# One-core diffusion backbone: attention threaded piece by piece through its projections, a third output unit ahead, idle products removed

## The chip, the cores and the metric

The program runs on one core of a Trainium2 chip. The metric is the time of one execution on the device in microseconds (us), median of several runs. TensorE multiplies matrices, VectorE and ScalarE do elementwise work, GpSimd is almost unused, and SyncE issues the loads. The profile calls them PE (with PEld for its weight loads), DVE, ACT, POOL and SP.

## The reference, cut to what matters

The model has two layers over 256 latent tokens and 256 context tokens of width 1024. Layer 0 is: half FFN, differential attention, half FFN; layer 1 has a Hyena convolution in the middle. Everything is float32. The change is inside the attention of layer 0:

```python
def attend(q, k, v):
    s = jnp.einsum('bqhmd,bkhmd->bhmqk', q, k).astype(jnp.float32)
    p = jax.nn.softmax(s, axis=-1)
    a = (p[:, :, 0] - lam_full * p[:, :, 1]).astype(v.dtype)
    return jnp.einsum('bhqk,bkhe->bqhe', a, v)
...
of = of * lax.rsqrt(jnp.mean(of * of, -1, keepdims=True) + LN_EPS)
of = of * subln_g.astype(jnp.float32) * (1.0 - lam_init)
return of.astype(o.dtype).reshape(b, n, DA_HEADS * DA_V_DIM) @ w_o
```

There are 8 heads, each with two softmaxes over 512 keys; queries and latent keys are rotated (rope). Only the 256 latent tokens have queries. After `w_o` comes a gated residual and a layer norm, then the next half FFN.

## The kernel before, in words

A float32 product is made of three TensorE products of rounded parts: each operand is split into a high part (ScalarE cast, `wH`, `qh`, `aH`) and a remainder (VectorE subtraction, `wL`, `ql`, `aL`), and high x high, high x low and low x high are summed in a PSUM bank. Weights come in units of 1 MB: two landing buffers (`raw`), three split units (`wH`/`wL`). `Stream` splits the next unit as soon as one is given back with `st.done`.

The attention works on two heads at a time, t = 0 to 3. For each t there are three projections, each with a weight unit of its own: queries (`pq`, 48 products of 256 columns), keys (`pka`, `pkb`, 48 products of 512 columns) and values (`pv`, 96 products of 256 columns). From them come, for each of two heads (hd) and two blocks of 128 queries (qt), a score block `sc`: two PSUM banks, one for each softmax, six products that use half of the array's rows each, so that two can run side by side. VectorE takes the row maximum (`mx`, L1035), ScalarE the exponential and its sum (`prob`, L1037), VectorE combines the two softmaxes (L1040 to L1044). The result is transposed on TensorE (`at`, L1062), split (`aH`, `aL`), multiplied with the values (`po`), squared and summed (`oss`), normed (`oe`, `odg`, and the product `orb` that spreads the factor over partitions), and split again (`oh`): two of the eight inputs of the output projection. That projection (`Project`, `py`) has four weight units of two output tiles each. Each tile is added to the residual `zl` (L1182), and `Norm` sums up the layer norm's statistics (`lnpm`, `lnd`, `lnq`, `lndl`, `lnst`, `lnrb`) tile by tile; `Norm.pilot` subtracts a first mean from all eight tiles as soon as the first tile is done.

The order inside a stage is not written out: the program is written in one order, and a list scheduler places each instruction by priority and by its own estimate of when operands are ready. On the chip each engine then runs its list strictly in that order. There are 7 PSUM banks for all of this and one more for `adaps` and `fill`. In the order of writing, all four score blocks of a t come as one call (`scores`), `values(t - 1)` takes parts of a projection between its steps (`part`, `V_BOUNDS`), and two units of the output projection are opened ahead.

`fill(n)` (L493) adds n products of a matrix of ones with itself, into a bank that nobody reads. It is called five times with n = 20: after each layer norm but the last. Being of low priority and waiting for nothing, all 100 were placed by the scheduler wherever it estimated TensorE to be free. Each is a float32 product that runs in two passes, so the trace has 200 records.

Of the kernel before, what the change touches and what calls it, by code (L numbers as in the profile page):

```python
# [33 lines left out]
ADA_LATER = 75  # L34
FILL = 20
# [15 lines left out]
V_BOUNDS = (0, 3, 5, 8)  # L51
# [253 lines left out]
def backbone(ctx, tc, A, out):  # L305
# [596 lines left out]
    fill(FILL)  # L902


    def attention(X, rope):
# [73 lines left out]
        def proj_qk(t, between=None):  # L979
            qi, pq, qo = q_outs()  # L980
            gemm(qo, XL, KT)
            st.done(qi)
            q_end(t, pq)
            if between:
                between()
            ki, pk, ko = k_outs()
            gemm(ko, X, KT)
            st.done(ki)
            k_end(t, pk)

        def proj_v(t):
            vi = st.get("w")
            pv = [bank("pv"), bank("pv")]
            v_mm(vi, pv, 0, KT)
            st.done(vi)
            v_end(t, pv)

        def first():
            qi, pq, qo = q_outs()
            ki, pk, ko = k_outs()  # L1000
            vi = st.get("w")
            pv = [bank("pv"), bank("pv")]
            ks = 5
            for k in range(ks):
                gemm(qo, XL, KT, k, k + 1)
                gemm(ko, X, KT, k, k + 1)
                v_mm(vi, pv, k, k + 1)
            gemm(qo, XL, KT, ks)
# [5 lines left out]
            v_mm(vi, pv, ks, KT)  # L1014
            st.done(vi)
            v_end(0, pv)

        def scores(t):
            qh, ql = Q.pop(t)
            kk = K.pop(t)  # L1020
            rec = sm(4, "rec")
            AA[t] = ([], rec)
            for hd in range(2):
                kh, kl = kk[hd]
                for qt in range(2):
                    ps = [bank("sc"), bank("sc")]
                    c = slice(T * hd + P * qt, T * hd + P * qt + P)
                    for n, (q2, k2) in enumerate(((qh, kh), (qh, kl), (ql, kh))):
                        for m in range(2):
                            r = slice(64 * m, 64 * m + 64)  # L1030
                            nc.tensor.matmul(ps[m], q2[r, c], k2[r, :], start=n == 0, stop=n == 2,  # L1031
                                             skip_group_check=True, tile_position=(64 * m, 0))
                    mx, sums, pr = sm(2, "mx"), sm(2, "sums"), []
                    for m in range(2):
                        V.tensor_reduce(mx[:, m:m + 1], ps[m], AX.X, OP.max, negate=True)  # L1035
                        p = blk("prob")
                        S.activation(p, ps[m], AF.Exp, bias=mx[:, m:m + 1], accum_out=sums[:, m:m + 1])  # L1037
                        pr.append(p)
                    r1 = sm(1, "r1")
                    V.reciprocal(r1, sums[:, 1:2])  # L1040
                    V.reciprocal(rec[:, 2 * hd + qt:2 * hd + qt + 1], sums[:, 0:1])
                    rr = sm(1, "rr")
                    V.tensor_scalar(rr, sums[:, 0:1], r1, nl, OP.mult, OP.mult)
                    V.scalar_tensor_tensor(pr[0], pr[1], rr, pr[0], OP.mult, OP.add)  # L1044
                    AA[t][0].append(pr[0])

        def values(t, between=()):

            pr, rec = AA.pop(t)
            vv = VV.pop(t)  # L1050
            between = list(between)
            ob = []
            ss = bank("oss")

            def turned(hd):
                aH = [blk("aH", F32R) for _ in range(2)]
                aL = [blk("aL", F32R) for _ in range(2)]
                for qt in range(2):
                    a = pr[2 * hd + qt]
                    pt = bank("at")  # L1060
                    for kt in range(4):
                        nc.tensor.transpose(pt[:, P * kt:P * kt + P], a[:, P * kt:P * kt + P], ident)  # L1062
                    c = slice(P * qt, P * qt + P)
                    for m in range(2):
                        split(aH[m].rearrange("p (k q) -> p k q", k=2)[:, :, c],
                              aL[m].rearrange("p (k q) -> p k q", k=2)[:, :, c],
                              pt[:, T * m:T * m + T].rearrange("p (k q) -> p k q", k=2))
                return aH, aL

            def weighted(hd, aH, aL):  # L1070
# [13 lines left out]
            def squares(hd):  # L1084
                for qt in range(2):
# [3 lines left out]
            def part():  # L1089
                if between:  # L1090
                    between.pop(0)()

            a0 = turned(0)
            part()
            weighted(0, *a0)
            a1 = turned(1)
            part()
            squares(0)
            weighted(1, *a1)
            part()  # L1100
            squares(1)
            e = sm(4, "oe")
            V.tensor_tensor(e, ss[:, 0:4], rec, OP.mult)
            V.tensor_tensor(e, e, rec, OP.mult)
            S.activation(e, e, AF.Sqrt, bias=epsc)
            V.reciprocal(e, e)
            V.tensor_tensor(e, e, rec, OP.mult)
            dg = blk("odg")
            for n in range(4):
                V.tensor_scalar(dg[:, P * n:P * n + P], ident, e[:, n:n + 1], None, OP.mult)  # L1110
            part()
            rb = bank("orb")
            mm(rb, ones, dg, True, True)
            for hd in range(2):
                o = ob[hd]
                V.scalar_tensor_tensor(o[:, :T], o[:, T:], g8, rb[:, T * hd:T * hd + T], OP.mult, OP.mult)
                oh = blk("oh", F32R)
                split(oh[:, :T], oh[:, T:], o[:, :T])
                O.append((oh[:, :T], oh[:, T:]))
            while between:  # L1120
                part()

        def v_parts(t, bounds):
            vi = st.get("w")
            pv = [bank("pv"), bank("pv")]

            def run(k0, k1):
                v_mm(vi, pv, k0, k1)
                if k1 == KT:
                    st.done(vi)  # L1130
                    v_end(t, pv)

# [284 lines left out]
```

## Time and profile before

| | |
|---|---|
| time, median of 3 runs | 1388.45 us (1387.35 to 1389.36) |
| the profiled execution's own time | 1387.11 us |
| its span | 1385.1 us |
| mean granted TensorE clock | 0.979 |
| TensorE busy | 1334.9 us, 96% of the span |
| VectorE, ScalarE busy | 1037.0 us, 662.0 us |

Times in the trace are microseconds from the start of the span. The attention's projections begin at 434.65 us, and the next FFN's first product starts at 652.68 us. Records of products overlap: a product of 256 columns is recorded with some 280 ns, but products follow each other every 0.12 us, and those of 512 columns every 0.23 us.

### The profile page before, as it was taken

The numbers are of one execution on the slowest core, as the hardware profiler recorded it, in microseconds if no ns is written. First come the engines' busy times: TensorE is split into PE (matmuls) and PEld (weight loads), VectorE is DVE, ScalarE is ACT, GpSimd is POOL, SyncE is SP. The second block draws the span as 40 slices with busy tenths as digits, with TensorE's granted clock in tenths as the row PEclk, the third lists the DMA queues.
The fourth block names the chain that finished last, engine by engine and source line by source line (L and its number), as shares of the span: only waits on it lengthen the run. The fifth ranks groups of instructions, "written<-read, shape, count | busy, mean of one in ns | idle before, by whom it ended". The sixth has DMA issues, their size and how long they took to land.

```text
span 1385.1 us, 19682 instructions
## 1 busy us (share of the span) xinstructions
PE 1334.9 (96%) x7624; PEld 1154.1 (83%) x7624; DVE 1037.0 (75%) x1919; ACT 662.0 (48%) x1175; POOL 12.3 (1%) x12
## 2 busy tenths in 40 slices
PE   7999999999999999997999999999999889999997
PEld 5688888888888888886888888888899889888886
DVE  3899988888967757668766667766668789776665
ACT  1443212222333846664755446655446444665533
POOL 0000000000000000000000000000000020000000
PEclk8999999999999999999999999999999999999999
DMA  9966788788841212112455454555653533255452
GB/s 308 378 243 243 275 332 348 307 326 331 305 145 44 92 61 92 62 62 92 160 206 182 146 189 153 213 183 175 202 201 138 211 108 122 106 198 184 164 173 88
DMA packets 44420, 261.41 MB, mean 189 GB/s; under 512 B 4964, under 2 KB 6692, under 8 KB 19624
## 3 DMA queue, kind: packets, MB, share of 16 engines
q1 hardware_dynamic: 44328, 260.16, 52.1%
q8 instruction: 60, 0.98, 0.3%
q14 instruction: 32, 0.26, 0.0%
HBM read 256.99 MB, written 3.15 MB: 188 GB/s over the span
## 4 chain that ended last, share of the span: by engine, by line
PE 89%; DVE 6%; ACT 3%; DMA 2%; issue 1%; ACTq 0%; SPq 0%
PE py L329 22%; PE pa L329 22%; PE pu L329 22%; PE pxv L329 5%; PE pv L329 2%; PE fill L329 2%; PE pq L329 2%; PE pka L329 2%; PE pkb L329 2%; DVE wL L233 1%; PE sc L1031 1%; ACT wH L232 1%; DMA raw<-wia 1%; PE hsp L329 1%; PE warm L329 1%
## 5 line engine op out<-in xcount | busy, mean ns | idle before, releaser
L233 DVE TENSOR_TENSOR wL<-raw,wH 128x1024 fp32r<-128x1024 f32 (+1 forms) x358 | 390.0, 1108 | 119.6 <-ACT wH L232 114.8
L232 ACT CAST wH<-raw 128x1024 fp32r<-128x1024 f32 (+1 forms) x358 | 330.7, 956 | 219.3 <-PE py L329 101.9
L329 PE MATMUL pa<-xhl,wH 128*128 128x512 f32 x520 | 190.4, 403 | 5.6 <-DVE xhl L813 5.6
L329 PE MATMUL pu<-xhl,wH 128*128 128x512 f32 x520 | 189.6, 402 | 0.0
L329 PE MATMUL py<-g,wH 128*128 128x512 f32 (+1 forms) x594 | 185.0, 370 | 0.0
L484 DVE SCALAR_TENSOR_TENSOR rawa<-rawa,condb 128x1024 f32<-128x1024 f32 x128 | 151.6, 1220 | 3.7 <-DMA rawa<-adr 3.2
L329 PE MATMUL py<-g,wL 128*128 128x256 f32 x528 | 147.2, 279 | 0.0
L329 PE MATMUL pa<-xhl,wL 128*128 128x256 f32 x520 | 146.8, 282 | 0.0
L329 PE MATMUL pu<-xhl,wL 128*128 128x256 f32 x520 | 146.8, 282 | 0.0
L329 PEld LDWEIGHTS pa<-xhl,wH 128*128 128x128 f32 x520 | 99.4, 191 | 30.3 <-DVE xhl L813 4.0
L329 PEld LDWEIGHTS py<-g,wH 128*128 128x128 f32 x594 | 107.1, 188 | 20.0
L329 PEld LDWEIGHTS pu<-xhl,wH 128*128 128x128 f32 x520 | 99.1, 191 | 24.3
L329 PEld LDWEIGHTS pa<-xhl,wL 128*128 128x128 f32 x520 | 99.8, 192 | 0.1
L329 PEld LDWEIGHTS py<-g,wL 128*128 128x128 f32 x528 | 99.6, 189 | 0.1
L329 PEld LDWEIGHTS pu<-xhl,wL 128*128 128x128 f32 x520 | 99.5, 191 | 0.0
L843 ACT ACTIVATE sil<-pa 128x512 f32<-128x512 f32 x22 | 13.2, 599 | 150.5 <-PE pa L329 150.5
L329 PE MATMUL pxv<-xhl,wH 128*128 128x256 f32 x384 | 75.7, 299 | 5.0 <-DVE pTl L510 3.8
L329 PEld LDWEIGHTS pxv<-xhl,wH 128*128 128x128 f32 x384 | 64.5, 206 | 5.7 <-DVE pTl L510 4.1
L329 PE MATMUL pa<-xh,wH 128*128 128x512 f32 x176 | 68.6, 390 | 0.0
L329 PE MATMUL pa<-xl,wH 128*128 128x512 f32 x176 | 68.5, 389 | 0.0
L329 PE MATMUL pu<-xh,wH 128*128 128x512 f32 x176 | 68.5, 389 | 0.0
L329 PE MATMUL pu<-xl,wH 128*128 128x512 f32 x176 | 68.5, 389 | 0.0
(316 smaller groups left out, 2647.9 us busy)
## 6 DMA issues: line engine op xcount, KB each, us to landing
rawa<-adr SPq DMA_DIRECT2D x64, 1024.0 KB, 7.1
raw<-wia SPq DMA_DIRECT2D x44, 1024.0 KB, 4.8
raw<-wib SPq DMA_DIRECT2D x44, 1024.0 KB, 4.8
raw<-woa SPq DMA_DIRECT2D x32, 704.0 KB, 4.2
raw<-wob SPq DMA_DIRECT2D x32, 704.0 KB, 4.1
rawa<-adx SPq DMA_DIRECT2D x8, 1024.0 KB, 8.2
raw<-wqk SPq DMA_DIRECT2D x8, 1024.0 KB, 4.7
raw<-whv SPq DMA_DIRECT2D x8, 1024.0 KB, 4.8
```

The costliest lines, as they stand in the source:

```text
L232: nc.scalar.copy(h[:, d], it["raw"][:, s:e])
L233: nc.vector.tensor_tensor(lo[:, d], it["raw"][:, s:e], h[:, d].bitcast(F32), OP.subtract)
L329: return nc.tensor.matmul(o, l, r, start=start, stop=stop, skip_group_check=True)
L484: V.scalar_tensor_tensor(junk if q else w, w, 1.0, condb[:, q, :], OP.mult, OP.mult, accum_out=mod[i][:, q, 2 * u + h:2 * u + h + 1])
L843: S.activation(s, pa, AF.Silu)
L1031: nc.tensor.matmul(ps[m], q2[r, c], k2[r, :], start=n == 0, stop=n == 2, skip_group_check=True, tile_position=(64 * m, 0))
```

## The change

The pieces are written one by one between small parts of the projections, by tables that give for each part the pieces that follow it: S0 to S3 are score blocks, T0 to T3 transposes, W0 and W1 weighted values, Q0 and Q1 sums of squares, N (or P for the t before) the norm. `thread` walks through the parts. At t = 3 the parts are those of the last value projection and of the output projection, of which a third unit is opened ahead and run through the first six inputs. `fill` and its five calls are gone.

```diff
-ADA_LATER = 75
-FILL = 20
-V_BOUNDS = (0, 3, 5, 8)
+PLAN = {1: "P", 3: "S0", 5: "S1", 7: "S2", 9: "S3 T0", 10: "T1", 11: "T2", 12: "W0", 14: "T3 Q0", 16: "W1", 18: "Q1"}
...
-    def fill(n):
-        with tc.high_priority(-ADA_LATER):
-            ps = adap.tile([P, 512], F32, name="fill", tag="ada")
-            for _ in range(n):
-                mm(ps[:, :P], ones, ones, True, True)
...
+            def q_part(k):
+                if k == 0:
+                    hold["q"] = q_outs()
+                qi, pq, qo = hold["q"]
+                gemm(qo, XL, KT, k, k + 2)
+                if k + 2 == KT:
+                    st.done(qi)
+                    q_end(t, pq)
...
+            qk = [lambda k=k: q_part(k) for k in range(0, KT, 2)] + [lambda k=k: k_part(k) for k in range(KT)]
+            return qk, [lambda k=k: v_part(k) for k in range(KT)]
...
-        def scores(t):
-            qh, ql = Q.pop(t)
-            kk = K.pop(t)
+        def scores(t, hd, qt):
+            qh, ql = Q[t]
+            kh, kl = K[t][hd]
...
+        def thread(main, plan, pieces, n0=0):
+            for n, part in enumerate(main):
+                part()
+                for name in plan.get(n0 + n, "").split():
+                    pieces[name]()
...
         st.spare(0)
-        first()
-        for t in range(1, 4):
-            proj_qk(t, (lambda: scores(0)) if t == 1 else None)
-            parts = v_parts(t, V_BOUNDS)
-            ahead = parts if t < 3 else parts[:1] + [lambda: None] * (len(parts) - 1)
-            values(t - 1, ahead + [lambda: scores(t)])
-            if t == 3:
-                for p in parts[1:]:
-                    p()
-        pj = Project(O, gate_cols(0, 5, 1, False))
-        pj.open(2)
-        values(3, [lambda a=a, b=b: pj.run(a, b) for a, b in ((0, 2), (2, 4), (4, 5), (5, 6))])
+        rest = first()
+        main, now = rest, {}
+        for t in range(4):
+            now = dict(value_pieces(t), P=now.get("N"))
+            if t < 3:
+                qk, v = qkv_parts(t + 1)
+                thread(main + qk, PLAN if t else PLAN_FIRST, now)
+                main = v
+            else:
+                pj = Project(O, gate_cols(0, 5, 1, False))
+                def pj_parts():
+                    pj.open(2)
+                    for k in range(6):
+                        yield lambda k=k: pj.run(k, k + 1)
+                    pj.open(1)
+                    for k in range(0, 6, 2):
+                        yield lambda k=k: pj.run(k, k + 2, 2)
+                thread(main, PLAN_LAST, now)
+                thread(pj_parts(), PLAN_LAST, now, KT)
         return pj.close(6)
...
-        def run(self, k0, k1):
-            gemm([o for g in self.grp for o in g[2]], self.O, KT, k0, k1)
+        def run(self, k0, k1, first=0):
+            gemm([o for g in self.grp[first:] for o in g[2]], self.O, KT, k0, k1)
```

What the scheduler makes of it is seen in the order of each engine. On TensorE at t = 0, where the score blocks of the first two heads follow the second query projection, the list before holds idle products between the score products of the second head (`sc_3596`, `sc_3597` are the two banks of one block):

```order
L329 MATMUL fill_7322<-ones_112 128x128 x2
L1031 MATMUL sc_3596<-kh_3413,qh_3355 128x512
L329 MATMUL fill_7322<-ones_112 128x128 x3
L1031 MATMUL sc_3596<-kl_3414,qh_3355 128x512
L1031 MATMUL sc_3596<-kh_3413,ql_3356 128x512
L329 MATMUL fill_7322<-ones_112 128x128
L1031 MATMUL sc_3597<-kh_3413,qh_3355 128x512
L1031 MATMUL sc_3597<-kl_3414,qh_3355 128x512
L1031 MATMUL sc_3597<-kh_3413,ql_3356 128x512
L329 MATMUL fill_7322<-ones_112 128x128 x9
L1031 MATMUL sc_3618<-kh_3413,qh_3355 128x512
```

In the list of the change the same place has no idle products, and the next key projection (`pka_3597`) follows the third score block:

```order
L1048 MATMUL sc_3511<-kh_3377,ql_3335 128x512
L1048 MATMUL sc_3512<-kh_3377,ql_3335 128x512
L1048 MATMUL sc_3575<-kh_3392,qh_3334 128x512
L1048 MATMUL sc_3575<-kl_3393,qh_3334 128x512
L1048 MATMUL sc_3575<-kh_3392,ql_3335 128x512
L1048 MATMUL sc_3576<-kh_3392,qh_3334 128x512
L1048 MATMUL sc_3576<-kl_3393,qh_3334 128x512
L1048 MATMUL sc_3576<-kh_3392,ql_3335 128x512
L334 MATMUL pka_3597<-xh_3071,wH_3326 128x512
```

The fourth block, which had 9 idle products ahead of it and 15 between its banks, now stands behind six products of the keys. On TensorE at t = 1, before, the last of four score blocks that stand together, with 16 idle products between its two banks (`sc_4005`, `sc_4006`), then the norm's product and the next query projection:

```order
L1031 MATMUL sc_4005<-kh_3713,qh_3533 128x512
L1031 MATMUL sc_4005<-kl_3714,qh_3533 128x512
L1031 MATMUL sc_4005<-kh_3713,ql_3534 128x512
L329 MATMUL fill_9181<-ones_112 128x128 x10
L329 MATMUL fill_10746<-ones_112 128x128 x6
L1031 MATMUL sc_4006<-kh_3713,qh_3533 128x512
L1031 MATMUL sc_4006<-kl_3714,qh_3533 128x512
L1031 MATMUL sc_4006<-kh_3713,ql_3534 128x512
L329 MATMUL orb_4027<-odg_3933,ones_112 128x512
L329 MATMUL pq_4037<-xh_3071,wH_3468 128x256
```

In the change a block of t = 2 (`sc_4381`, `sc_4382`), each block standing alone between parts of the value projection:

```order
L334 MATMUL pv_4275<-wL_3957,xh_3120 128x256
L334 MATMUL pv_4275<-wH_3956,xl_3121 128x256
L1048 MATMUL sc_4381<-kh_4240,qh_4095 128x512
L1048 MATMUL sc_4382<-kh_4240,qh_4095 128x512
L1048 MATMUL sc_4381<-kl_4241,qh_4095 128x512
L1048 MATMUL sc_4382<-kl_4241,qh_4095 128x512
L1048 MATMUL sc_4381<-kh_4240,ql_4096 128x512
L1048 MATMUL sc_4382<-kh_4240,ql_4096 128x512
L334 MATMUL pv_4274<-wH_3956,xh_3130 128x256
L334 MATMUL pv_4274<-wL_3957,xh_3130 128x256
```

The two banks of a block alternate again in 15 of the 16 blocks; before, in 6 of them one bank was finished ahead of the other. On VectorE at the end of the attention, before, both halves of the weight unit `wL_5282` are split ahead of the layer norm's small steps (`lnb`, `lnrs`, `lndg`):

```order
L1182 SCALAR_TENSOR_TENSOR zl_3033<-py_5294,gate05_4980,zl_3033 128x256
L233 TENSOR_TENSOR wL_5282<-raw_5190,wH_5281 128x1024 x2
L775 TENSOR_SCALAR lnb_5369<-lnb_5369 128x2
L782 RECIPROCAL lnrs_5375<-lnrs_5375 128x2
L786 TENSOR_SCALAR lndg_5380<-ident_86,lnrs_5375 128x128
L786 TENSOR_SCALAR lndg_5383<-ident_86,lnrs_5375 128x128
```

In the change the halves of the same unit (`wL_5261`) stand between those steps:

```order
L1202 SCALAR_TENSOR_TENSOR zl_3033<-py_5273,gate05_4746,zl_3033 128x256
L773 TENSOR_SCALAR lnb_5348<-lnb_5348 128x2
L238 TENSOR_TENSOR wL_5261<-raw_5206,wH_5260 128x1024
L780 RECIPROCAL lnrs_5354<-lnrs_5354 128x2
L238 TENSOR_TENSOR wL_5261<-raw_5206,wH_5260 128x1024
L784 TENSOR_SCALAR lndg_5359<-ident_86,lnrs_5354 128x128
L784 TENSOR_SCALAR lndg_5362<-ident_86,lnrs_5354 128x128
```

ScalarE's casts of that unit moved likewise, from ahead of the statistics to the places between them. From the next FFN's first product on, the lists of all engines are the same as before.

## Rows read from the trace of the kernel before

**Rows 1.** From the page: each engine's busy time, share of the span, instructions.

```profile
PE 1334.9 (96%) x7624; PEld 1154.1 (83%) x7624; DVE 1037.0 (75%) x1919; ACT 662.0 (48%) x1175; POOL 12.3 (1%) x12
```

**Rows 2.** From the page: the chain that ended last, by line.

```profile
PE py L329 22%; PE pa L329 22%; PE pu L329 22%; PE pxv L329 5%; PE pv L329 2%; PE fill L329 2%; PE pq L329 2%; PE pka L329 2%; PE pkb L329 2%; DVE wL L233 1%; PE sc L1031 1%; ACT wH L232 1%; DMA raw<-wia 1%; PE hsp L329 1%; PE warm L329 1%
```

**Rows 3.** Busy time by stretch: length, PE, PEld, DVE, ACT, POOL, PEclk, DMA.

```profile
434.60:628.10 193.50, 186.94 (x1289) 166.49 (x1287) 132.09 (x301) 120.08 (x255) 0.00 (x0) 1.00 0.18 66
```

**Rows 4.** The same stretch, the records of fill alone (PE, PEld).

```profile
434.60:628.10 193.50, 19.86 (x153) 17.77 (x151) 1.00 0.18 66
```

**Rows 5.** PE timeline, holes of the attention: start, us, what, count, [idle].

```profile
469.64 2.62 PE L329 MATMUL fill<-ones 128*128 128x128 f32 x22
...
560.89 0.39 PE L1031 MATMUL sc<-kh,ql 64*128 64x512 f32 x2
561.12 0.39 PE L1031 MATMUL sc<-kh,qh 64*128 64x512 f32 x1
...
561.89 3.39 PE L329 MATMUL fill<-ones 128*128 128x128 f32 x28
565.21 0.49 PE L1031 MATMUL sc<-kh,qh 64*128 64x512 f32 x1
```

**Rows 6.** Timeline of PE, the layer norm ahead of the attention.

```profile
425.04 0.91 PE L329 MATMUL fill<-ones 128*128 128x128 f32 x6
425.79 1.57 PE L329 MATMUL lnst<-o,lnsq 128*128 128x1 f32 x8
...
434.65 0.36 PE L329 MATMUL pq<-xh,wH 128*128 128x256 f32 x1
```

**Rows 7.** Timeline of DVE, the same layer norm.

```profile
428.36 0.87 DVE L786 TENSOR_SCALAR lndg<-ident,lnrs 128x128 f32<-128x128 f32 x4
...
431.88 1.28 DVE L805 TENSOR_TENSOR z<-z,lnrb 128x512 f32<-128x512 f32 x2 [1.27 <-PE lnrb L329]
```

**Rows 8.** Busy time by stretch: PEclk is the number behind the engines' pairs.

```profile
426.00:428.00 2.00, 2.00 (x8) 1.70 (x8) 0.00 (x0) 0.60 (x4) 0.00 (x0) 0.50 0.00 0
626.00:630.00 4.00, 2.95 (x14) 1.85 (x14) 2.04 (x5) 0.80 (x2) 0.00 (x0) 1.00 0.00 0
654.00:658.00 4.00, 4.00 (x15) 3.41 (x14) 4.00 (x13) 3.44 (x7) 0.00 (x0) 0.50 0.00 0
658.00:660.00 2.00, 2.00 (x13) 1.72 (x12) 2.00 (x7) 1.43 (x4) 0.00 (x0) 0.99 0.05 12
```

**Rows 9.** Timeline of DVE, t = 0: keys of the two heads, last step.

```profile
470.27 0.43 DVE L510 TENSOR_TENSOR kl<-ru,kh 128x256 fp32r<-128x256 f32 x1 [0.90 <-ACT kh L509]
...
475.34 0.41 DVE L510 TENSOR_TENSOR kl<-ru,kh 128x256 fp32r<-128x256 f32 x1
```

**Rows 10.** Groups by shape, 434.6 to 628.1 us: count, busy, mean ns.

```profile
L232 ACT CAST wH<-raw 128x1024 fp32r<-128x1024 f32 x22 | 22.5, 1048 | 5.9 <-PE pq L329 5.5
...
L1035 DVE TENSOR_REDUCE mx<-sc 128x1 f32<-128x512 f32 x32 | 20.8, 681 | 8.5 <-PE sc L1031 8.5
```

**Rows 11.** Timeline of PE, from the norm of t = 3 on.

```profile
626.04 1.12 PE L329 MATMUL orb<-odg,ones 128*128 128x512 f32 x2 [1.42 <-DVE odg L1110]
...
628.17 0.85 PE L329 MATMUL py<-oh,wH 128*128 128x256 f32 x3 [1.01 <-ACT oh L509]
```

**Rows 12.** The chain of waits to the next FFN: start, us, what.

```profile
635.80 0.80 DVE zl L1182 x2
...
636.64 5.79 PE py L329 x46
...
643.08 3.12 PE py L329 x24
...
646.63 2.35 DVE wL L233 x2
...
650.14 0.73 PE lnrb L329 x4
...
652.68 1.01 PE pa L329 x2
```

More of the change, by code (lines that the diff above doesn't have):

```diff
@@ L977, in v_end, with qkv_parts, k_part, v_part @@
                 VV[t].append((h, lo))
[L979 to L996, printed above, removed]
+        def qkv_parts(t):
+            hold = {}
+            def q_part(k):
[6 more added lines that the diff above has]
+                    q_end(t, pq)
+            def k_part(k):
+                if k == 0:
+                    hold["k"] = k_outs()
+                ki, pk, ko = hold["k"]
+                gemm(ko, X, KT, k, k + 1)
+                if k + 1 == KT:
+                    st.done(ki)
+                    k_end(t, pk)
+            def v_part(k):
+                if k == 0:
+                    hold["v"] = st.get("w"), [bank("pv"), bank("pv")]
+                vi, pv = hold["v"]
+                v_mm(vi, pv, k, k + 1)
+                if k + 1 == KT:
+                    st.done(vi)
+                    v_end(t, pv)
+            qk = [lambda k=k: q_part(k) for k in range(0, KT, 2)] + [lambda k=k: k_part(k) for k in range(KT)]
+            return qk, [lambda k=k: v_part(k) for k in range(KT)]
         def first():
@@ L1047, in values, with rest @@
[L1047 to L1070, printed above, removed]
+            def rest(k):
+                v_mm(vi, pv, k, k + 1)
+                if k + 1 == KT:
+                    st.done(vi)
+                    v_end(0, pv)
@@ new lines, in first @@
+            return [lambda k=k: rest(k) for k in range(ks, KT)]
+        def scores(t, hd, qt):
+            qh, ql = Q[t]
+            kh, kl = K[t][hd]
+            if (hd, qt) == (0, 0):
+                AA[t] = ([], sm(4, "rec"))
+            pr_, rec = AA[t]
+            ps = [bank("sc"), bank("sc")]
+            c = slice(T * hd + P * qt, T * hd + P * qt + P)
+            for n, (q2, k2) in enumerate(((qh, kh), (qh, kl), (ql, kh))):
+                for m in range(2):
+                    r = slice(64 * m, 64 * m + 64)
+                    nc.tensor.matmul(ps[m], q2[r, c], k2[r, :], start=n == 0, stop=n == 2,
+                                     skip_group_check=True, tile_position=(64 * m, 0))
+            mx, sums, pr = sm(2, "mx"), sm(2, "sums"), []
+            for m in range(2):
+                V.tensor_reduce(mx[:, m:m + 1], ps[m], AX.X, OP.max, negate=True)
+                p = blk("prob")
+                S.activation(p, ps[m], AF.Exp, bias=mx[:, m:m + 1], accum_out=sums[:, m:m + 1])
+                pr.append(p)
+            r1 = sm(1, "r1")
+            V.reciprocal(r1, sums[:, 1:2])
+            V.reciprocal(rec[:, 2 * hd + qt:2 * hd + qt + 1], sums[:, 0:1])
+            rr = sm(1, "rr")
+            V.tensor_scalar(rr, sums[:, 0:1], r1, nl, OP.mult, OP.mult)
+            V.scalar_tensor_tensor(pr[0], pr[1], rr, pr[0], OP.mult, OP.add)
+            pr_.append(pr[0])
@@ new lines, in value_pieces, with turned, weighted @@
+        def value_pieces(t):
+            ob, sides, hold = [], {}, {}
+            def turned(hd, qt):
+                if qt == 0:
+                    sides[hd] = [blk("aH", F32R) for _ in range(2)], [blk("aL", F32R) for _ in range(2)]
+                aH, aL = sides[hd]
+                a = AA[t][0][2 * hd + qt]
+                pt = bank("at")
+                for kt in range(4):
+                    nc.tensor.transpose(pt[:, P * kt:P * kt + P], a[:, P * kt:P * kt + P], ident)
+                c = slice(P * qt, P * qt + P)
+                for m in range(2):
+                    split(aH[m].rearrange("p (k q) -> p k q", k=2)[:, :, c],
+                          aL[m].rearrange("p (k q) -> p k q", k=2)[:, :, c],
+                          pt[:, T * m:T * m + T].rearrange("p (k q) -> p k q", k=2))
+            def weighted(hd):
+                aH, aL = sides.pop(hd)
+                vv = VV[t]
@@ L1084, in squares @@
             def squares(hd):
+                if hd == 0:
+                    hold["ss"] = bank("oss")
+                ss = hold["ss"]
                 for qt in range(2):
@@ L1106, in values @@
[L1106 to L1119, printed above, removed]
@@ L1120, in values @@
-            while between:
-                part()
[L1123 to L1131, printed above, removed]
-            return [lambda a=a, b=b: run(a, b) for a, b in zip(bounds[:-1], bounds[1:])]
-        st.spare(0)
-        first()
-        for t in range(1, 4):
-            proj_qk(t, (lambda: scores(0)) if t == 1 else None)
-            parts = v_parts(t, V_BOUNDS)
-            ahead = parts if t < 3 else parts[:1] + [lambda: None] * (len(parts) - 1)
-            values(t - 1, ahead + [lambda: scores(t)])
-            if t == 3:
-                for p in parts[1:]:
-                    p()
@@ new lines, in squares, with normed @@
+                dg = hold["dg"] = blk("odg")
+                for n in range(4):
+                    V.tensor_scalar(dg[:, P * n:P * n + P], ident, e[:, n:n + 1], None, OP.mult)
+            def normed():
+                rb = bank("orb")
+                mm(rb, ones, hold["dg"], True, True)
+                for hd in range(2):
+                    o = ob[hd]
+                    V.scalar_tensor_tensor(o[:, :T], o[:, T:], g8, rb[:, T * hd:T * hd + T], OP.mult, OP.mult)
+                    oh = blk("oh", F32R)
+                    split(oh[:, :T], oh[:, T:], o[:, :T])
+                    O.append((oh[:, :T], oh[:, T:]))
```

68 lines of the change are left out of this document (19 added, 49 removed).

## The prediction

> **What bounds the kernel now.** I read the page's busy line first. TensorE is busy 96% of the span, VectorE 75%, ScalarE 48% [rows 1]. The chain of waits says the same: its large pieces are products (`py`, `pa`, `pu`), and `fill`, which computes nothing, holds 2% of it [rows 2], against 1% for a load. So the kernel is a queue on TensorE, and time is won where that queue gets shorter or where TensorE stands still without showing it. Then I took the stretch that the change rewrites, from the first query projection (434.65) to the first product that needs the last normed output (628.17). In its 193.5 us TensorE is busy 186.94, VectorE 132.09, ScalarE 120.08, at full clock, with the transfers at 18% [rows 3]. Of TensorE's busy time 153 records are idle products [rows 4]. The timeline gives what one is worth: 28 of them lie between two score products that start 3.32 us apart, 0.119 each [rows 5]. (The 19.86 of [rows 4] can't be used as it stands, since records overlap.) So 153 x 0.119 = 18.2 us of idle products, 193.5 - 186.94 = 6.6 us of holes, and 168.7 us of real work. The two waits of the last norm, 1.42 and 1.01, are in those holes [rows 11].
>
> An idle product that fills a wait costs nothing, and one that delays real work costs its length. The list scheduler put them where it estimated TensorE free. On the chip, 22 stand at 469.64, where the first head's keys are ready at 470.27 + 0.43 = 470.70 [rows 5, 9]: 22 x 0.119 = 2.6 us of products for 1.1 us of wait. The others I can only judge by what waits are there without them, so the sum is real work plus waits.
>
> **The change, part by part**, against the profiled execution (1387.11; the median of the runs lies 1.34 above it).
>
> *Layer norm ahead of the attention.* Six idle products stand ahead of the statistics, `lnst` [rows 6]: without them these start some 0.7 earlier, and more of them before the clock falls (426 to 428 us ran at 0.50, the lower of the two levels, idle products notwithstanding [rows 8]). The four steps `lndg` end at 428.36 + 0.87 = 429.2, but `z` waited 1.27 for `lnrb` and began at 431.88 [rows 7]: idle products and half-clock products stand between. With `lndg` 1.7 earlier and `lnrb` next to it, `z` begins near 428.8: -3.1. Against it, TensorE then restarts from rest. At the next layer norm, which has no idle products near its end, the first `pa` comes at 652.68 [rows 12], and the clock is at 0.50 until 658 and at 0.99 after it [rows 8]: 5.3 us at half, 2.6 us lost. Bounds: -3.1 (the clock comes back as it does now) to +3.5 (the statistics gain nothing and a longer stretch runs at half). I take -3.1 + 2.6 = -0.5: the projections start as if at 434.15.
>
> *Real work to the last norm.* 168.7, plus the third output unit's 36 products, which move ahead of the norm at 0.12 each (products of 256 columns [rows 11]): +4.3. Six score blocks ran bank after bank, now one does. With the banks alternating, two score products run side by side in one step of 0.23 (two at 560.89, the next at 561.12 [rows 5]); within one bank each takes a step of its own. So a block costs 3 x 0.23 = 0.7 or 6 x 0.23 = 1.4: 5 x -0.7 = -3.5. Transposes stand in 16 places alone rather than together. No row shows what such a stop costs. Between 0 and one step of 0.23 for each (3.7) I take 2, the middle. Sum 171.5.
>
> *Waits that come in.* At t = 0 the second query projection must still be followed by scores. The first block waits 1.1 us as above. The second head's last key step ended at 475.34 + 0.41 = 475.75 [rows 9], while two blocks are through at about 470.7 + 1.4 = 472.1: at most 3.6, and I take 2.2, as VectorE has fewer steps ahead of it in the new order. 0.6 more is for banks, one maximum being 0.68 [rows 10]. Together about 4. At t = 1 to 3 each block stands alone between projection parts, and one block's two maxima (1.4) fit beside a part. The waits are between 0 and 10 (three holes like the 3.32 of [rows 5], which `fill` hid). I take 2: VectorE has 132 us of work in the now 177 us, so it is the nearest engine to a bound and not one. The waits of the last norm (1.42, 1.01) lie beside 24 of the third unit's products, 2.9 us: nothing. So the product that needs the last `oh` comes at 434.15 + 171.5 + 6 = 611.7 instead of 628.17: -16.5.
>
> *Tail of the output projection.* Before, from there to the last `py` (643.08 + 3.12 = 646.2 [rows 12]) it took 18.0. The 4.3 us of the third unit are gone from it, but VectorE holds its order: residuals, the eight subtractions of the first mean, residuals, sums. At 635.80 TensorE waited for the residual `zl`, before the last 48 + 24 products could go [rows 12]. The fourth unit is the one that has to wait, for a weight buffer and for its low half on VectorE (two steps of about 1.2 for one unit [rows 12]), and it can't be split before the first output unit is given back. By VectorE's list the third unit's residuals end 8.4 after the restart, the fourth unit's split at 9.9, and 48 products with one residual between them take 6.9: 16.8. So of 4.3 only -1.2 comes through. Bounds: -4.3 to 0.
>
> *Layer norm behind it.* Before, two halves of `wL` (2.35) stand ahead of `lnb`, beside the statistics on TensorE; `lnrb` comes 650.14 - 646.20 = 3.9 after the last `py` [rows 12]. Now they stand between `lnb`, the reciprocal and `lndg`, each a step of one chain: 2.35 more on it, 0.35 less in front. ScalarE's casts (1.05 each [rows 10]) stand likewise between the roots. +2.0; bounds 0 and +4.1 (both casts as well).
>
> *Idle products elsewhere.* 200 - 153 = 47 records, 29 of them in the norm above or beside it; 18 are worth at most 2.1. They stand before products that wait for VectorE anyway: -0.3. Behind the attention nothing moves.
>
> **Sum:** -16.5 - 1.2 + 2.0 - 0.3 = -16.0; 1387.1 - 16.0 = 1371.1, and 1.3 more for the median: 1372.4.
>
> **A rule that speaks against it.** The Trainium skill, TensorE: Matmul & The Clock Gate, section "A second HAM failure mode: psum-queue depth-cycling", says that short idle spells between groups of products, as banks are cycled through, make the clock swing between its levels. By that, threaded blocks without idle products would lose more than their waits. This trace bears it out only in part: 426 to 428 ran at half with products in it [rows 8], yet 626 to 630, with TensorE busy 2.95 of 4 us, stayed at full. It is rival D, whose numbers come from rows.
>
> **Rivals.**
> A, the forecast: idle products were mostly longer than the waits they stood in. Its own range is 1367.5 to 1378: waits of t = 1 to 3 from 0 to 7, the norm's start 3 either way.
> B, the waits come back. All 18.2 us of idle products stood in real waits for exponentials, maxima and norms, and the thread does not cover them. Then 171.5 + 18.2 = 189.7, the last norm is 4.3 earlier, and with the tail's +0.5 the time is 1387.1 - 3.8 + 1.3 = 1384.6. For it: the holes beside which `fill` stood, such as 28 records between two banks of one block. Against: in those 3.32 us the scheduler had other products to place and chose by its estimate, not by the chip's times; and the blocks now stand apart, with projection parts between.
> C, VectorE does not hold the tail: the third unit brings all its 4.3 and the norm is not longer by 2: 1372.4 - 3.1 - 2.0 = 1367.3. For it: VectorE is at 2.04 of 4 us at 626 to 630 [rows 8]. Against: the wait at 635.80 is for VectorE.
> D, slower: without idle products the clock falls in the score stretches of the attention. Each us at half loses half a us, so it decides from 32 us at half upward; with 10 us at each of four t the loss is 20, and the time 1372.4 + 20 = 1392.4. For it: 426 to 428 and 654 to 658 [rows 8]. Against: the stretch of 626 to 630 with its 1.42 and 1.01 us of waits at 1.00, and a hole is expected to be no longer than these but for the 2.2 at t = 0.
> That the blocks are regrouped by the scheduler, so that nothing is threaded, is ruled out by TensorE's list but for three blocks of t = 0.
>
> **How the numbers follow.** A 0.60, C 0.18, B 0.14, D 0.08. The time is A's, 1372. The range runs from 1364 (C with no wait at t = 1 to 3 and a full-clock start: 1367.3 - 2 - 2.6 = 1362.7, not all of it) to 1381 (A with 10 us of waits there: 1380.4); it leaves out B and D. What a measurement of this kernel can tell from no change is 0.2%, 2.8 us: faster means below 1385.7. A and C lie below it, B with two thirds of its chance: 0.60 + 0.18 + 0.09 + a rest of D = 0.88; same 0.05; slower 0.07.
>
> **What would show it.** In the profile of the changed kernel: no `fill` records. The stretch from the first `pq` to the product after the last `oh` is about 178 us rather than 193.5; its idle time is some 6 us, over half of it near the first scores; a larger idle time there is B. The granted clock of that stretch is 1.00 but for its first 5 us; another value is D. `z` of the norm ahead of it begins near 429. From the product on the last `oh` to the last `py`: 16.8 (13.7 would be C). From there to `lnrb`: 5.9. If the first is right and the stretch still isn't shorter, the sum of idle products was the wrong place to look.

## The result, and the profile after

The changed kernel takes 1370.22 us (median of 4 runs, 1370.05 to 1371.63), against 1387.9 for the kernel before in the same comparison: a ratio of 0.9881, 95% interval 0.9855 to 0.9908. The forecast was 1372, range 1364 to 1381. The profiled execution has a span of 1368.1 us, 17.0 less.

The page of the changed kernel, the lines that answer to [rows 1, 2]:

```profile
PE 1312.9 (96%) x7424; PEld 1129.7 (83%) x7424; DVE 1037.2 (76%) x1919; ACT 660.0 (48%) x1175; POOL 12.3 (1%) x12
...
PE py L334 24%; PE pa L334 22%; PE pu L334 22%; PE pxv L334 5%; PE pv L334 2%; DVE wL L238 1%; ACT wH L237 1%; PE hsp L334 1%; PE pka L334 1%; PE pkb L334 1%; PE warm L334 1%; DMA raw<-wia 1%; PE lnst L334 1%; PE po L334 1%; ACT rsw L925 1%
```

`fill` is gone from the chain, and `py` has 2% more of it. The page cannot say what made the time shorter. For that the way from the layer norm ahead of the attention to the next FFN is cut at the same six places in every trace (starts, from the timeline): the last product ahead of the norm, the first `pq`, the first product on the last `oh`, the last `py`, `lnrb`, and the next FFN's first `pa`.

| us | norm ahead | projections and scores | tail | to `lnrb` | to `pa` | sum |
|---|---|---|---|---|---|---|
| before | 13.5 | 193.5 | 17.7 | 4.2 | 2.5 | 231.6 |
| changed | 9.7 | 179.2 | 18.0 | 5.8 | 3.0 | 215.8 |
| no_idle_alone | 9.7 | 196.0 | 18.9 | 4.2 | 2.5 | 231.3 |
| thread_with_idle | 13.5 | 178.2 | 19.9 | 5.2 | 2.4 | 219.3 |
| two_units_ahead | 9.7 | 179.1 | 18.9 | 4.2 | 2.5 | 214.4 |
| idle_in_tail | 9.7 | 179.2 | 16.8 | 5.8 | 3.0 | 214.5 |
| second_head_later | 9.7 | 178.8 | 17.2 | 5.8 | 3.0 | 214.5 |
| split_after_norm | 9.7 | 179.2 | 18.0 | 3.4 | 2.5 | 212.9 |
| all_mended | 9.7 | 178.8 | 16.8 | 3.4 | 2.5 | 211.3 |
| two_ahead_held_clock | 9.7 | 179.6 | 17.7 | 4.2 | 2.5 | 213.8 |

So 15.7 of the 17.0 us lie here. Whole runs of one kernel differ by several us (1382.69 to 1394.02 for the kernel before, over 17 runs), so the small effects below are read from this table. It has one trace of each kernel. Where two kernels share a stretch and the granted clock is alike in it, they agree within 0.2 us. Where it is not, they differ by about 1 us, though TensorE's products are the same: the tail with two units ahead takes 17.7 or 18.9. Two more examples, with the columns of [rows 3], where the clock is the number behind the engines' pairs. From the first `pq` to the last one ahead of the scores, the changed kernel and then second_head_later:

```profile
430.51:466.61 36.10, 35.99 (x240) 33.31 (x240) 29.21 (x57) 24.77 (x45) 0.00 (x0) 0.95 0.20 63
```

```profile
434.89:471.89 37.00, 37.00 (x239) 34.46 (x240) 29.24 (x58) 25.62 (x48) 0.00 (x0) 0.91 0.20 70
```

The tail of second_head_later (the changed kernel's is the fifth row of the next list):

```profile
613.70:631.13 17.43, 13.56 (x87) 12.50 (x88) 15.03 (x33) 7.10 (x13) 0.00 (x0) 0.90 0.16 61
```

So a difference of about 1 us in the table is an effect of an edit only where the granted clock is compared too.

Windows of the changed kernel, with the columns of [rows 3]; the first answers to it:

```profile
430.51:609.65 179.14, 175.65 (x1172) 152.50 (x1172) 134.62 (x304) 120.19 (x258) 0.00 (x0) 0.98 0.20 71
432.00:434.00 2.00, 2.00 (x9) 1.64 (x8) 2.00 (x6) 0.51 (x2) 0.00 (x0) 0.50 0.00 0
434.00:436.00 2.00, 2.00 (x11) 1.71 (x10) 2.00 (x6) 0.58 (x2) 0.00 (x0) 0.66 0.00 0
474.00:476.00 2.00, 2.00 (x6) 1.50 (x5) 1.93 (x7) 1.95 (x5) 0.00 (x0) 0.50 0.01 4
609.69:628.00 18.31, 14.61 (x87) 13.46 (x88) 15.12 (x33) 7.11 (x13) 0.00 (x0) 0.81 0.16 58
618.00:620.00 2.00, 1.53 (x7) 1.42 (x7) 2.00 (x5) 1.95 (x4) 0.00 (x0) 0.50 0.00 0
```

TensorE is idle for 179.14 - 175.65 = 3.5 us of the stretch, against 6.6 before. But the clock fell in three places where it had been at full: at the start (432 to 435), behind the first scores (474), and in the tail (618).

Timeline of TensorE in the changed kernel, with the columns of [rows 5, 6]: the end of the norm, and t = 0.

```profile
427.48 1.56 PE L334 MATMUL lnrb<-lndg,ones 128*128 128x128 f32 x8
...
430.51 0.39 PE L334 MATMUL pq<-xh,wH 128*128 128x256 f32 x1 [1.47 <-ACT xh L809]
...
471.19 0.49 PE L1048 MATMUL sc<-kh,qh 64*128 64x512 f32 x1 [1.46 <-ACT kh L507]
```

The first `pq` now comes 3.0 us behind `lnrb`, with no idle product between, and 1.46 us are lost where the second head's keys are late.

The chain of waits of the changed kernel, from the last `oh` on, answering to [rows 11, 12]:

```profile
609.69 2.16 PE py L334 x15
...
616.03 1.49 PE py L334 x6
...
618.47 5.76 PE py L334 x28
...
628.00 0.43 PE lndl L334 x2
...
630.84 1.22 DVE wL L238
...
632.14 1.17 DVE wL L238
...
633.56 1.24 PE lnrb L334 x4
...
636.61 1.01 PE pa L334 x2
```

The two halves of `wL` stand between the norm's steps, as VectorE's list had them, and `lnrb` at half clock takes 1.24 where it took 0.73.

### The profile page after: what moved, and what is told of

It is laid out like the page before. It is cut to its first block, busy times and chain, and to the rows that moved or that the text cites. A ratio compares the mean times of both kernels' runs of the same rounds, so it can differ in the third digit from the quotient of the medians.

```text
span 1368.1 us, 19280 instructions
## 1 busy us (share of the span) xinstructions
PE 1312.9 (96%) x7424; PEld 1129.7 (83%) x7424; DVE 1037.2 (76%) x1919; ACT 660.0 (48%) x1175; POOL 12.3 (1%) x12
## 4 chain that ended last, share of the span: by engine, by line
PE 84%; DVE 9%; ACT 4%; issue 2%; DMA 1%; ACTq 0%; SPq 0%; DVEq 0%
PE py L334 24%; PE pa L334 22%; PE pu L334 22%; PE pxv L334 5%; PE pv L334 2%; DVE wL L238 1%; ACT wH L237 1%; PE hsp L334 1%; PE pka L334 1%; PE pkb L334 1%; PE warm L334 1%; DMA raw<-wia 1%; PE lnst L334 1%; PE po L334 1%; ACT rsw L925 1%
## 5 line engine op out<-in xcount | busy, mean ns | idle before, releaser
L334 PE MATMUL py<-g,wH 128*128 128x512 f32 (+1 forms) x594 | 188.1, 374 | 0.0
L334 PE MATMUL pa<-xh,wL 128*128 128x512 f32 x176 | 68.5, 389 | 0.0
L334 PE MATMUL pu<-xh,wL 128*128 128x512 f32 x176 | 68.5, 389 | 0.0
```

The lines of the kernel that those rows point to most:

```text
L334: return nc.tensor.matmul(o, l, r, start=start, stop=stop, skip_group_check=True)
```

## The experiments

### The idle products alone, and the threading alone

**no_idle_alone**: the kernel before, without the calls.

```diff
-    fill(FILL)
```
(all five)

> The kernel before with its idle products removed and nothing threaded. Forecast's reason (idle products were mostly longer than the waits they stood in, and threading takes away most of what waits remain): the layer norm ahead of the attention starts the projections about 4 us earlier, the score blocks of t = 0 to 2 still stand four together, and their waits for maxima and banks return in part. About 1379 us, some 9 of the 17 us. Rival (all idle products stood in real waits, the threading does the work): 1384 to 1387. Second rival (threading and the third unit bring nothing, the removal is all): 1371.

Measured: 1386.9 us, ratio to before 0.9997 (0.9973 to 1.0021): nothing, where 1379 was expected, and inside the first rival's 1384 to 1387. The norm ahead became 3.8 us shorter, and the stretch behind it 2.5 and the tail 1.2 longer. TensorE's timeline in this kernel: the third and fourth score blocks at t = 0, and the fourth block's second bank at t = 1 and 2.

```profile
471.38 0.49 PE L1030 MATMUL sc<-kh,qh 64*128 64x512 f32 x1 [1.45 <-ACT kh L509]
...
475.08 0.76 PE L1030 MATMUL sc<-kh,qh 64*128 64x512 f32 x1 [1.46 <-DVE ru L930]
...
478.29 0.79 PE L1030 MATMUL sc<-kh,qh 64*128 64x512 f32 x1 [1.60 <-ACT prob L1036]
...
517.12 0.49 PE L1030 MATMUL sc<-kh,qh 64*128 64x512 f32 x1 [3.04 <-ACT prob L1036]
...
561.43 0.50 PE L1030 MATMUL sc<-kh,qh 64*128 64x512 f32 x1 [3.04 <-ACT prob L1036]
```

Windows of the same kernel: the stretch, and at t = 1 the hole and what follows it.

```profile
430.70:626.69 195.99, 179.18 (x1136) 155.88 (x1137) 133.82 (x305) 121.71 (x258) 0.00 (x0) 0.94 0.19 65
514.00:518.00 4.00, 0.95 (x4) 0.48 (x3) 4.00 (x12) 3.96 (x8) 0.00 (x0) 1.00 0.00 0
518.00:522.00 4.00, 4.00 (x16) 3.04 (x16) 3.96 (x12) 3.52 (x11) 0.00 (x0) 0.57 0.29 72
```

The 28 records of [rows 5] stood in a wait of 3.04 us for an exponential to give a bank free. Without them TensorE stands still there, and behind the hole the clock is granted at 0.57 for 4 us. Over the stretch that is 195.99 - 179.18 = 16.8 us of idle time, where the kernel before had 18.2 of idle products and 6.6 of holes. By that count 16.8 - 6.6 = 10.2 us of the idle products stood in real waits, and 8.0 were longer than their waits. But the clock over the stretch is 0.94 instead of 1.00, and the stretch became 2.5 us longer, not 8.0 shorter: the lower clock took all of it and more. So neither "mostly longer than their waits" nor rival B's "all in real waits" is right, and what the idle products brought was in good part the full clock, rival D's mechanism, in the kernel that is not threaded.

**thread_with_idle**: the changed kernel with the five calls put back.

```diff
+    fill(FILL)
```
(behind each of the five norms)

> The changed kernel with the five calls of idle products put back: everything is threaded, the scheduler places the 100 products anew. 17 of them stand in the first score stretch of t = 0, about 39 in the tail of the output projection, 14 around the next layer norm, the rest ahead of the attention as before. If idle products cost their length wherever they stand: 39 x 0.24 = 9 us in the tail less the 3 us that TensorE stands still there, 3 us in the norm ahead of the attention, so about 1370 + 9 = 1379. Rival (they keep the granted clock up where it fell in the changed kernel, at 472 to 477 and 616 to 623, and so pay for themselves): 1370 to 1373.

Measured: 1372.27 us, 0.9893 (0.9872 to 0.9914), inside the rival's range and not the 1379. The timeline of TensorE: idle products at t = 0, and the longest pieces in the tail.

```profile
467.48 2.62 PE L336 MATMUL fill<-ones 128*128 128x128 f32 x22
...
472.81 0.47 PE L1058 MATMUL sc<-kh,qh 64*128 64x512 f32 x1 [0.47 <-DVE vl L517]
...
620.77 2.84 PE L336 MATMUL fill<-ones 128*128 128x128 f32 x24
...
626.47 1.50 PE L336 MATMUL fill<-ones 128*128 128x128 f32 x12
```

The windows: the stretch up to the product on the last `oh`, and the place at t = 0 that ran at half clock in the changed kernel.

```profile
432.49:610.67 178.18, 176.77 (x1223) 155.78 (x1222) 133.52 (x303) 119.57 (x256) 0.00 (x0) 1.00 0.21 72
474.00:478.00 4.00, 4.00 (x19) 2.44 (x19) 3.92 (x13) 3.40 (x9) 0.00 (x0) 1.00 0.00 2
```

With idle products in the holes the clock is 1.00 throughout, and the stretch takes 178.2 us, 1.0 less than without them. In the tail they cost 1.9, not the 6 of the expectation (9 less 3), and in the norm ahead 3.8. So the threading brings 15 to 17 us of the stretch, with idle products (193.5 to 178.2) or without (196.0 to 179.2). Taking these out brings about 3.4 to the next FFN's first product once the work is threaded, and nothing measurable without it. Behind that product a part is given back. The windows of the first 20 products of the next FFN, in the changed kernel and in this one:

```profile
636.61:641.80 5.19, 5.19 (x20) 4.49 (x21) 5.19 (x17) 4.05 (x9) 0.00 (x0) 0.66 0.15 65
```

```profile
638.22:641.85 3.63, 3.63 (x20) 3.17 (x21) 3.63 (x12) 2.83 (x6) 0.00 (x0) 1.00 0.06 23
```

With idle products in the norm the FFN starts at full clock, and 1.6 us of the 3.4 are gone again.

### The third output unit, and the tail

**two_units_ahead**: the third unit is not opened ahead, and the norm follows the sixth input.

```diff
-             13: "Q1", 15: "N"}
+             13: "Q1 N"}
...
-                    pj.open(1)
-                    for k in range(0, 6, 2):
-                        yield lambda k=k: pj.run(k, k + 2, 2)
```

> The changed kernel with two units of the output projection opened ahead instead of three; the norm of t = 3 then follows the last input that can run. Reason now held: the third unit only moves 4.3 us of products out of a tail that VectorE bounds, where TensorE then stands still and its clock falls to half (616 to 623 us). So the product on the last oh comes about 4.3 - 2.2 = 2 us earlier (the norm's two waits of 1.4 and 1.0 are open again), the tail takes about 18 us as it did with three, at full clock: 1368. Rival (the third unit covers the norm and is worth its 4 us): 1373 to 1374.

Measured: 1371.48 us, 0.9885 (0.9857 to 0.9912), which can't be told from the changed kernel; the cut stretches say 214.4, 1.4 less than with the third unit. The last norm on TensorE's timeline in this kernel:

```profile
610.46 2.05 PE L334 MATMUL orb<-odg,ones 128*128 128x512 f32 x2 [2.19 <-DVE odg L1117]
...
613.52 1.04 PE L334 MATMUL py<-oh,wH 128*128 128x256 f32 x3 [1.01 <-ACT oh L507]
```

The waits ahead of `orb` and `oh` are open (2.19 and 1.01), and the clock fell, so `orb` took 2.05 instead of 1.0. That eats the 4.3 us that went: the stretch is as long as with three units, not the 2 us shorter that was expected. Behind it the tail is 0.9 longer, at a clock of 0.90, where the same products took 17.7 at full clock in the kernel before. The norm and the way to `pa` are 2.1 shorter, because the split of a weight unit comes early enough again not to stand between its steps. By the cut stretches the rival (three units are worth 4 us) fails. Whole runs decide nothing: their interval holds both 1368 and 1373.

**idle_in_tail**: 24 products that nobody reads, in the tail only.

```diff
+                    if self.jj == 3 and self.idle:
+                        with tc.high_priority(-75):
+                            ps, h = adap.tile([P, 512], F32, name="idle", tag="ada"), self.O[KT - 1][0]
+                            for _ in range(self.idle):
+                                mm(ps[:, :T], h[:, :P], h, True, True)
```

> The changed kernel with 24 products of 256 columns that nobody reads, in the tail of the output projection only (8 and 16, where TensorE stood still for 0.9, 1.2 and 1.0 us waiting for the fourth unit and for residuals). If the half clock from 616 to 623 us comes of that standing still and costs time: the granted clock stays at 1.00 there, and the tail from the product on the last oh to the last py takes about 16 us instead of 18.3: 1368. Rival (VectorE bounds the tail and the half clock lies beside it): tail 18 us, 1370; if the idle products delay the real ones, 1371 to 1372.

Measured: 1367.44 us, 0.9866 (0.984 to 0.9893). Windows of the tail in this kernel, answering to the changed kernel's 18.31 at 0.81 and its 618 to 620 at 0.50:

```profile
611.11:628.14 17.03, 14.78 (x111) 13.89 (x112) 15.02 (x33) 7.11 (x13) 0.00 (x0) 1.00 0.16 61
617.00:619.00 2.00, 1.91 (x16) 1.70 (x15) 1.77 (x6) 0.98 (x3) 0.00 (x0) 1.00 0.00 0
```

The clock stays at 1.00, and the tail is 17.0 to the end of the last `py`, near the 16.8 of the forecast. So at full clock the tail is about 17 us, in line with VectorE's order, and what came on top in the changed kernel was the half clock: the same tail took 18.3 at a clock of 0.81, 17.4 at 0.90 in second_head_later, and 17.0 at 1.00 here. That is 1.3 us won, where 2.3 were expected (about 16 instead of 18.3).

### What is left over

**second_head_later**: at t = 0 the second head's blocks two key parts later.

```diff
-PLAN_FIRST = {3: "S0", 4: "S1", 6: "S2", 7: "S3", 8: "T0", 9: "T1", 11: "T2 W0", 12: "T3 Q0", 13: "W1", 14: "Q1"}
+PLAN_FIRST = {3: "S0", 4: "S1", 8: "S2", 9: "S3 T0", 10: "T1", 11: "T2 W0", 12: "T3 Q0", 13: "W1", 14: "Q1"}
```

> The changed kernel with the score blocks of the second head at t = 0 (S2, S3) written two key parts later, and the pieces behind them one part later. In the changed kernel TensorE waits 1.46 us for the second head's keys and runs at half clock from 473 to 477. If that wait and the half clock behind it are what is left of t = 0: the stretch from the first query projection to the product on the last oh is 179.2 - 1.5 - 1.5 = 176.2 us. Rival (the wait only moves, since the blocks come closer to their transposes, or the clock falls elsewhere): 179 us. Times of whole runs differ by several us outside the attention, so the stretch in the trace decides.

Measured: 1370.71 us, 0.9883 (0.9856 to 0.9911); the stretch is 178.8, not 176.2, near the rival's 179. But 0.9 us of it were lost ahead of the edited place, where this trace ran at 0.91 and the changed kernel's at 0.95 (the windows above). Behind that place the stretch is 1.3 us shorter than in the changed kernel: 178.8 - 37.0 against 179.2 - 36.1. So neither holds whole: of the 3.0 expected 1.3 came. The wait of 1.46 is gone and the clock at 472 to 484 is 1.00, but TensorE's timeline has two other waits:

```profile
475.13 0.47 PE L334 MATMUL pka<-xh,wH 128*128 128x512 f32 x1 [1.02 <-DVE vl L508]
...
492.70 0.38 PE L334 MATMUL po<-aL,vh 128*128 128x256 f32 x1 [0.94 <-DVE aL L508]
```

The key projection itself waits for a bank that the value projection's split gives free (`vl`), and the weighted values come close behind their operands.

**split_after_norm**: the split of the next FFN's third unit waits until the norm is through.

```diff
-                        st.done(it, j == KT - 1)
+                        st.done(it, j >= self.late)
...
+        pj.late = KT - 3
         return pj.close(6)
```

> The changed kernel with the split of the next FFN's third weight unit held back until the layer norm behind the attention is through. Its casts and subtractions then no longer stand between the norm's small steps: lnrb comes 4.2 us after the last py as before instead of 5.8, and the next FFN's first product 2.5 later instead of 3.0 if the clock is full there: 2 us less. Rival: the third unit is then late for the next FFN and TensorE waits there, by 2 us or more, so nothing is won or it is slower.

Measured: 1370.51 us, 0.9872 (0.9843 to 0.9902). TensorE's timeline, the norm's `lnrb` and the FFN's first products:

```profile
631.99 0.71 PE L334 MATMUL lnrb<-lndg,ones 128*128 128x128 f32 x4 [0.51 <-DVE lndg L784]
...
634.52 0.76 PE L334 MATMUL pa<-xhl,wH 128*128 128x512 f32 x1 [1.82 <-DVE xhl L811]
...
639.81 0.50 PE L334 MATMUL pa<-xhl,wH 128*128 128x512 f32 x1 [0.60 <-DVE xhl L811]
...
642.45 0.50 PE L334 MATMUL pa<-xhl,wH 128*128 128x512 f32 x1 [0.96 <-DVE xhl L811]
```

To `pa` it is 2.9 us shorter (2 expected), and in the FFN two waits of 0.60 and 0.96 are new, which the changed kernel does not have. Both theories hold in part. The net is 1.4 by these rows, below what whole runs can show.

**all_mended**: the three edits together (`idle_in_tail`, `second_head_later`, `split_after_norm`).

```diff
+        pj.idle, pj.late = 24, KT - 3
         return pj.close(6)
```
(with `PLAN_FIRST` as above)

> The changed kernel with all three edits that are tried singly: second head's blocks later, 24 products that nobody reads in the tail, and the split held back until the norm is through. If the three are independent: from the first query projection to the next FFN's first product 206.1 us now, less 3.0, 1.3 and 2.0 = 199.8, and 1364 us. Rival (holding back the split costs in the FFN what it wins): 1366.

Measured: 1371.5 us, 0.988 (0.9851 to 0.991). The cut stretches sum to 211.3, 4.5 below the changed kernel, where 6.3 was expected. 0.9 of what is missing went ahead of the edits, as in second_head_later: up to the last `pq` ahead of the scores this trace too took 37.0 us, at 0.91. Whole runs do not show the 4.5: 1366.9 to 1376.74. I can't name a version that is measurably faster than the changed kernel.

**two_ahead_held_clock**: two units ahead, `PLAN_FIRST` as above, and 24 idle products ahead of the last `orb`.

```diff
+                if t == 3:
+                    with tc.high_priority(-75):
+                        ps, h = adap.tile([P, 512], F32, name="idle", tag="ada"), O[KT - 3][0]
+                        for _ in range(24):
+                            mm(ps[:, :T], h[:, :P], h, True, True)
```

> Two output units ahead, the second head's blocks at t = 0 later, and 24 products that nobody reads ahead of the last norm's orb, where TensorE waited 2.2 us and the clock then fell. If the clock is held there, orb takes 1.0 instead of 2.1 us, and the tail is at full clock: from the first query projection to the product on the last oh 179.0 - 3.0 - 1.1 - 0.6 = 174.3, tail 17.7, lnrb 4.2 behind it, sum to the next FFN 198.8, 1363 us. Rival (three units ahead with a held clock is better): sum over 200.

Measured: 1369.68 us, 0.9871 (0.9848 to 0.9893). The last norm on TensorE's timeline:

```profile
608.11 3.12 PE L334 MATMUL idle<-oh 128*128 128x256 f32 x24
...
611.07 1.02 PE L334 MATMUL orb<-odg,ones 128*128 128x512 f32 x2
...
613.10 0.84 PE L334 MATMUL py<-oh,wH 128*128 128x256 f32 x3 [1.01 <-ACT oh L507]
```

`orb` is back at 1.02 and the tail at full clock, as expected. The stretch is not 174.3 but 179.6: the edit at t = 0 gave waits again, the window from 494 to 496 us ran at 0.50, and the 24 idle products (3.12 us) are longer than the wait of 2.19 in which they stand. From the first query projection to the next FFN it is 204.1 (213.8 less the norm ahead), over 200 as the rival said. That does not show that three units are better: all_mended has 201.6 there, but it also holds back the split. Three units at a held clock without that, idle_in_tail, have 204.8.

## Why the prediction was right, and where its steps were wrong

**The sum.** To the next FFN's first product it gave -15.7 with 1387.1 as its base, and 652.68 - 636.61 = 16.1 were measured. It was right because it was built as real work plus waits: 171.5 us of work were forecast for the stretch, and 179.14 less 3.5 idle and 3.4 lost to the clock (1.7 at its start, 1.7 at t = 0) is 172.2. That the total came within 0.4 us is luck: the product on the last `oh` came 2.0 us earlier than forecast (609.69 against 611.7), most of it from the norm ahead, and the tail took 1.5 us more.

**Idle products "mostly longer than the waits they stood in".** Wrong as a statement on the kernel before: 8.0 of 18.2 us were, by no_idle_alone, and the clock took them back, so that alone their removal brings nothing (0.9997). The sample it rested on, 2.6 us of products for 1.1 us of wait at 469.64, was read rightly but is not typical: just behind it, and at t = 1 and 2, they stood in waits of 1.5 to 3.0 us. (The 3.32 us at 561.89 run from the first of the 28 idle products to the score product behind them, not between two score products; the 0.119 for each stands.) The objection to rival B, that the scheduler chose by its own estimate, held for less than half of them. What B missed is that threaded work covers these waits. The forecast's number did not depend on the statement, because threading was priced as waits of 2 us at t = 1 to 3.

**Waits.** 6 us were forecast; 3.5 us of idle time came and, at t = 0, 1.7 us of lost clock (0.72, 0.50 and 0.92 in the three windows of 2 us from 472), which was no term of the sum. Together 5.2. As foreseen, over half of the idle time (0.61 and 1.46) is at the first scores. Rival D's mechanism is there in one short piece of the score stretches instead of 40 us.

**The norm ahead.** Forecast 3.1 earlier and 2.6 lost to the clock. Measured 3.8 earlier in the cut stretch, and 0.50 from 432 to 434 and 0.66 from 434 to 436, 1.7 us: 2.1 gained where 0.5 was forecast. `z` began at 429.08, near the 429 foreseen. What the sum left out is that idle products also stood right ahead of the first `pq`. TensorE's timeline before, and VectorE's in the changed kernel:

```profile
431.63 3.26 PE L329 MATMUL fill<-ones 128*128 128x128 f32 x20
```

```profile
429.08 1.28 DVE L803 TENSOR_TENSOR z<-z,lnrb 128x512 f32<-128x512 f32 x2
```

So `z` came 2.8 earlier (431.88 to 429.08) and `pq` 4.1 (434.65 to 430.51). How much of the projections runs at half clock differs between traces of the same products (0.95 and 0.91 above), so a part of the 1.7 is chance.

**The tail.** Forecast 16.8, measured 18.3: the step that failed most. "VectorE holds its order" was right (17.0 in idle_in_tail at full clock), but that TensorE, which then stands still, would fall to half clock was not priced, although the forecast for the start of the projections had that very term. In the sum the third unit lost 2.7 us on balance (4.3 - 2.4 - 1.2, and 2.0 in the norm behind); against two_units_ahead it lost 1.4, in two traces with half clock at different places, so the size is not sure.

**The norm behind.** Forecast 5.9 from the last `py` to `lnrb`, measured 633.56 - 628.00 = 5.6; before it was 3.9. From there to `pa` it took 3.0 instead of 2.5, with `lnrb` at half clock, so 2.1 is what came, as forecast. Holding the split back (split_after_norm) wins 2.9, more than came in.

**The rule of the Trainium skill** (TensorE: Matmul & The Clock Gate, "A second HAM failure mode: psum-queue depth-cycling"), which was weighed against the change, is borne out by no_idle_alone: banks that come free late, holes of 3.04 us, and 0.57 granted behind them. In the threaded kernel the clock falls behind a wait in two places: at 474 behind a wait for keys (1.46), not for a bank, and in the tail.

## What to carry to other kernels

An idle product on the busiest engine says nothing about time by itself: find the wait it stands in by taking it out alone, and put real work there before taking it away. Price each new hole of TensorE twice, once for its length and once for the half clock that may follow it: holes of 1.46 and 3.04 us were followed by half clock here, while the 1.42 and 1.01 at 626 to 630 in the kernel before and the 1.02 and 0.94 in second_head_later were not. In two_ahead_held_clock the same edit left waits at the same two places, and half clock followed the second (0.50 from 494 to 496), so the length of a hole alone did not decide it. Work moved out of a stretch that another engine bounds was not won here; it left a hole there. Before a difference of 1 us is put down to an edit, compare the granted clock in stretches that the edit does not touch.

## What was not expected of the hardware

Two executions at full granted clock, with TensorE busy throughout, ran the same FFN products at different rates. The changed kernel and two_units_ahead, 100 us of the next FFN, where their lists are the same; first the windows, then the group of one product (count, busy, mean ns), each for the one and the other:

```profile
660.00:760.00 100.00, 100.00 (x578) 88.15 (x578) 70.06 (x112) 59.80 (x110) 0.00 (x0) 1.00 0.54 188
```

```profile
663.00:763.00 100.00, 100.00 (x568) 86.77 (x567) 69.27 (x109) 59.99 (x110) 0.00 (x0) 1.00 0.53 187
```

```profile
L334 PE MATMUL pa<-xhl,wH 128*128 128x512 f32 x144 | 50.7, 391 | 0.0
```

```profile
L334 PE MATMUL pa<-xhl,wH 128*128 128x512 f32 x144 | 51.7, 399 | 0.0
```

At 1.00 the one gets through more products in 100 us than the other, and a product of 512 columns is 2% longer. From this norm's `lnrb` to the next the one takes 194.3 us and the other 197.0. Whole runs of one kernel differ by a few times that; whether this is the cause wasn't tested. What sets the rate stays open: the granted clock does not show it.
